# Hybrid decoder step: the second parts of the compression's rows come last, one operand pair lies lowest, one store moves to SP

## The chip, the core and the metric

The kernel runs on one core of a Trainium2 chip. The metric is the device time of one execution in microseconds (us), the median of several runs. Within the core, TensorE (PE) multiplies, VectorE (DVE), ScalarE (ACT) and GpSimd (POOL) work on rows, and SyncE (SP) issues transfers (DMA). PE has a queue of its own for loading weights, shown as PEld. Each engine takes its instructions in order and waits for semaphores of others.

## The reference

One layer of a hybrid decoder for 512 prompt tokens and 8 samples of 8 new tokens with 4096 earlier positions each. What matters here:

```python
def compress(rows, w1, b1, w2, b2, pos):          # rows -> compressed keys or values
    ch = rows[:, :nch * 16].reshape(B, nch, 16, N_KV, HEAD_DIM)
    h_first  = einsum('bcpgd,pdh->bcgh', ch, w1[:16])
    h_second = einsum('bcpgd,pdh->bcgh', ch, w1[16:])
    h = h_first[:, :-1] + h_second[:, 1:] + (einsum('pd,pdh->h', pos, w1) + b1)
    return einsum('bcgh,hd->bcgd', silu(h), w2) + b2

q, k_cmp, v_cmp, ..., gates, z_att, u, z_ssm, g_merge = split(x @ w_in)
kc, vc = compress(all_k, ...), compress(all_v, ...)      # prompt and samples
o_att = gated sum of: attention to kc/vc, to 16 selected blocks, to the window
y = gelu(S5(u));  s = (y @ glu_w[0] + b0) * sigmoid(y @ glu_w[1] + b1)
merged = sigmoid(g_att) * ((o_att * silu(z_att)) @ w_att_out) \
       + sigmoid(g_ssm) * ((s * silu(z_ssm)) @ w_ssm_out)
x = layer_norm(ALPHA * x + merged @ w_o)
```

All is float32. The kernel gets this precision on PE by splitting an operand into a first part (rounded, names ending in h) and a second part (the rest, names ending in l), and adding three products: first x first, second x first, first x second.

## The kernel before

The input projection and the S5 branch come first. Then the prompt's attention is done in four tiles of 128 tokens (`prompt_tile`, i = 0 to 3), and beside the later ones the compression of the samples' cached rows begins. Then four windows of two samples each attend (`attend`, w = 0 to 3), with the rest of the compression beside windows 0 to 2. The gated linear unit and the output projection of the S5 branch (`ssm_out`) run beside window 3. The attention's projection, `w_o` and the layer norm (`output`) end the kernel.

**Compression.** POOL gathers cached rows by page (`gc`, L1091), DVE transposes them (`xt`, L892), and `first_layer` multiplies them by the weights `w1`. It is called for 16 half-blocks x 2 (keys, values), and each call makes four steps, 128 in all. A step splits a quarter of the rows: ACT copies the first part `evh` (L108, in `split`), DVE subtracts to get the second part `evl` (L121). There are two buffers of each (`self.evs`), used in turn. Then come 12 products into the accumulator `p_mm`, three for each of four (r, f), in the order of `mm3`: `evh` with `w1h` (L129), `evl` with `w1h` (L130), `evh` with `w1l` (L131). SiLU (`hs`, `hth`) and the second layer (`p_ca`, L1165 and L1173) follow each block, with `kc` and `vc` as the results.

**Prompt tile.** Scores `p_S`, softmax `P`, transposes `p_tr` of `P` (L135), ACT's copies `pt`, products `p_acc` (L1036, L1078). At the end DVE multiplies the accumulator by the gate rows, `ast` (L1084), and the rows are stored to `aD` in DRAM (L1085), which a later load reads back. `attend_setup` follows: `kn`, and a load of a constant `selt` by SP (L1217), which the products of the gates need (L1220).

**Output part.** `ssm_out` takes 32 loads of `y` (issued by SP, held behind `selt`'s load by `issue_after`), splits `y` into four pairs `ah`, `al` (ACT, DVE) and the weights `or` into `oh`, `ol`, and multiplies. Its pool "out" lies where buffers of the compression lay before. Buffers get their addresses in the order in which they are first asked for: `z`, `ring`, then the pairs 0 to 3. So a pair may have to wait for what was there: pair 0 lies over the last `hth` and the rows `gc`, pair 3 above it.

**What sets the order.** The program is written as generators that are woven by hand, but a planner then reorders all instructions on all engines by its own model of times, within the limits of data and buffers. So a small edit can move instructions all over the program, and the order of what runs must be looked at as it comes out.

Of the kernel before, what the change touches and what calls it, by code (L numbers as in the profile page):

```python
# [85 lines left out]
def rr(ap, pat, **kw):  # L86
    return ap.rearrange(pat, **kw)


class Hybrid:  # L90
# [899 lines left out]
    def prompt_tile(self, i, KT, kczs, vcp, bt):  # L990

        nc, pp = self.nc, self.pp
# [4 lines left out]
        q0 = i * 128  # L997
        n = q0 + 128
        bv = bt[:]
        acc = self.psum("acc", [128, 512])  # L1000
        gr = self.grp
        for br in range(2):
# [21 lines left out]
            for kt in range(i + 1):  # L1024
# [10 lines left out]
                for g in range(2):  # L1035
                    mm = nc.tensor.matmul(acc[gr[g]], self.kvn[:, kt, c0 + g * 64:c0 + (g + 1) * 64], PTs[g][:], start=br == 0 and kt == 0,  # L1036
                                          stop=False, skip_group_check=True)
# [44 lines left out]
        st = pp.tile([128, 4, 128], F, name="ast", tag="ast", bufs=1)  # L1082
        nc.sync.dma_start(st[:], rr(self.zD[0:4], "r p t -> p r t")[:, :, q0:q0 + 128])
        V.tensor_tensor(st[:], rr(acc[:], "p (r q) -> p r q", r=4), st[:], op=OP.mult)  # L1084
        nc.scalar.dma_start(self.aD[:, :, q0:q0 + 128], st[:])  # L1085


    def gather(self, out, cache, idx):
# [55 lines left out]
    def first_layer(self, kv, h, x, acc):  # L1144

        for k2 in range(4):
            self.evn += 1
            xt = self.evs[self.evn % 2]
            self.split(xt[0][:, :, :, 1:129], xt[1][:, :, :, 1:129], x[:, 2 * k2:2 * k2 + 2])
            for r in range(2):  # L1150
                for f in range(2):
                    wj = 8 * f + 2 * k2 + r
                    to, at, n = (126, 0, 130) if h and f else (128 * h, 1 + f, 128)
                    self.mm3(acc[:, :, to:to + n], (self.w1s[kv][0][:, wj, :], self.w1s[kv][1][:, wj, :]),
                             (xt[0][:, r, :, at:at + n], xt[1][:, r, :, at:at + n]),
                             h == 0 and wj == 0, h == 1 and wj == 15, skip_group_check=True)
            yield

    def second_layer(self, kv, sl, out):
# [366 lines left out]
    def ssm_out(self):  # L1526

        nc, A, pd = self.nc, self.A, self.pd
        V, G = nc.vector, nc.gpsimd
        TT, TS, ST = V.tensor_tensor, V.tensor_scalar, V.scalar_tensor_tensor  # L1530
        self.halves = [slice(h * 288, h * 288 + 288) for h in range(2)]

        self.scratch("z")
        self.ring()
        for ct in range(4):
            self.pair(ct)
        self.weight_tiles()
        bg = pd.tile([128, 2, 4], F, name="bg")
        with nc.allow_non_contiguous_dma("bias"):
            nc.sync.dma_start(bg[:], rr(A["ssm_glu_b"], "k (t p) -> p k t", p=128))  # L1540
        TS(bg[:, 1], bg[:, 1], 0.5, None, op0=OP.mult)
        gh, gl = [], []
        for ct in range(4):
            y = self.py.tile([128, TOK], F, name="y", tag="y", bufs=4)
            ys = rr(self.yD[ct * 8:ct * 8 + 8], "g (t c) n -> g c t n", t=8)
            for g in range(8):
                with self.tc.issue_after(self.selt_dma.ins):
                    nc.sync.dma_start(rr(y[g * 16:(g + 1) * 16], "c (t n) -> c t n", t=8), ys[g])
            hi, lo = self.pair(ct)
            self.split(rr(hi, "p (n t) -> p t n", t=8), rr(lo, "p (n t) -> p t n", t=8), rr(y[:], "p (t n) -> p t n", t=8))  # L1550
            gh.append(hi)
            gl.append(lo)

        sh, sl = [], []
        gw = rr(A["ssm_glu_w"], "k (t p) c -> p k t c", p=128)
        for ct in range(4):
            c = slice(ct * 128, (ct + 1) * 128)
            hi, lo = self.weights([(gw[:, 0, :, c], 4), (gw[:, 1, :, c], 4)])
            z, th, ln = self.scratch("z"), self.scratch("th"), self.scratch("ln")
            nc.sync.dma_start(z[:], self.zD[4 + ct])  # L1560
            for s in self.halves:
                for k in (1, 0):
                    p = self.bank()
                    for t in range(4):
                        self.mm3(p[:, :288], (hi[:, 4 * k + t], lo[:, 4 * k + t]), (gh[t][:, s], gl[t][:, s]), t == 0, t == 3)
                    if k:
                        self.act(th[:, s], p[:, :288], AF.Tanh, scale=0.25, bias=bg[:, 1, ct:ct + 1])
                    else:
                        self.act(ln[:, s], p[:, :288], AF.Identity, scale=0.5, bias=bg[:, 0, ct:ct + 1])
                    yield  # L1570
            ST(ln[:], th[:], 1.0, ln[:], op0=OP.add, op1=OP.mult)
            G.tensor_tensor(ln[:], ln[:], z[:], op=OP.mult)
            hi, lo, _ = self.ring()
            self.split(hi, lo, ln[:])
            sh.append(hi)
            sl.append(lo)

        ws = rr(A["w_ssm_out"], "(t p) c -> p t c", p=128)
        self.merged = []
        for c2 in range(4):  # L1580
            self.merged += self.ring(F)[0:2]
            hi, lo = self.weights([(ws[:, :, (2 * c2 + u) * 128:(2 * c2 + u + 1) * 128], 4) for u in range(2)])
            for u in range(2):
                ct = 2 * c2 + u
                if ct == 0:
                    self.glu_dma = self.wdma
                tg = self.scratch("tg")
                nc.sync.dma_start(tg[:], self.gD[8 + ct])
                for s in self.halves:
                    p = self.bank()  # L1590
                    for t in range(4):
                        self.mm3(p[:, :288], (hi[:, 4 * u + t], lo[:, 4 * u + t]), (sh[t][:, s], sl[t][:, s]), t == 0, t == 3)
                    ST(self.merged[ct][:, s], tg[:, s], 1.0, p[:, :288], op0=OP.add, op1=OP.mult)
                    yield
# [136 lines left out]
```

## Time and profile before

| what | value |
|---|---|
| time, median of 3 runs | 892.15 us (891.99 to 892.65) |
| profiled execution, its time | 889.58 us |
| profiled execution, span from first to last instruction | 887.8 us |
| PE busy | 849.6 us, 96% |
| DVE busy | 568.8 us, 64% |
| ACT busy | 426.2 us, 48% |
| mean granted TensorE clock | 0.981 of full speed |

The profile shows one execution. Busy times are sums over the span; PE's products are pipelined, so a product's own duration is longer than the distance to the next one. All start times below are microseconds from the start of the span. The time and the span differ by 1.8 us, which lie around the program.

### The profile page before, as it was taken

How to read it: one execution, taken by the hardware profiler on the slowest of the kernel's cores; microseconds unless marked ns; L12 is line 12 of the kernel's file. 1: busy time of each engine (PE TensorE's matmuls, PEld its weight loads, DVE VectorE, ACT ScalarE, POOL GpSimd, SP SyncE). 2: the span in 40 equal slices, each digit the busy share in tenths (PEclk: the TensorE clock that was granted, in tenths of full speed). 3: DMA queues.
4: the chain of work that ended last, by engine and by line, in shares of the span. 5: the costliest groups of instructions: out<-in, count | busy, mean ns of one | idle time of the engine just before them, and what ended most of it. 6: DMA issues, size and time to landing. Idle time of an engine off the chain costs nothing.

```text
span 887.8 us, 18479 instructions
## 1 busy us (share of the span) xinstructions
PE 849.6 (96%) x7276; PEld 747.8 (84%) x7276; DVE 568.8 (64%) x1559; ACT 426.2 (48%) x876; POOL 196.0 (22%) x249
## 2 busy tenths in 40 slices
PE   8999999999999988999989999999999979999996
PEld 8999999999999967787757878787878758889885
DVE  3469973855354479988627767766764463448784
ACT  4224462223254365768535656555555565545420
POOL 0322719300042211121211323241321101200000
PEclk9999999999999979999979999999999989999999
DMA  8385526365687352323457746383726164849331
GB/s 279 95 201 165 148 67 193 113 203 150 208 247 239 135 133 96 120 96 120 148 182 216 264 164 261 120 313 116 285 97 238 61 236 145 283 129 277 109 107 48
DMA packets 116039, 151.03 MB, mean 170 GB/s; under 512 B 29352, under 2 KB 93224, under 8 KB 111600
## 3 DMA queue, kind: packets, MB, share of 16 engines
q1 hardware_dynamic: 89072, 65.02, 25.6%
q0 software_dynamic: 17824, 80.16, 25.2%
q10 hardware_dynamic: 9056, 4.67, 1.8%
q8 instruction: 57, 0.93, 0.4%
q14 instruction: 30, 0.25, 0.1%
HBM read 134.02 MB, written 19.93 MB: 173 GB/s over the span
## 4 chain that ended last, share of the span: by engine, by line
PE 65%; DVE 11%; DMA 7%; issue 5%; POOL 4%; ACT 4%; SPq 3%; POOLq 0%; DVEq 0%; ACTq 0%
PE p_mm L130 11%; PE p_mm L129 10%; PE p_mm L131 10%; PE p_tr L135 7%; PE p_S L1237 4%; PE p_ca L129 3%; PE p_ca L131 3%; PE p_ca L130 3%; DVE xt L892 2%; PE p_acc L1246 2%; DMA gc<-in_cache_kv_cmp,idx 2%; PE p_acc L1036 2%; DMA relx<-in_rel_bias 1%; DMA wraw<-in_w_in 1%; DVE evl L121 1%
## 5 line engine op out<-in xcount | busy, mean ns | idle before, releaser
L130 PE MATMUL p_mm<-evl,w1h 128*128 128x256 f32 (+1 forms) x512 | 153.8, 300 | 6.3 <-DVE evl L121 6.2
L129 PE MATMUL p_mm<-evh,w1h 128*128 128x256 f32 (+1 forms) x512 | 151.1, 295 | 1.1 <-ACT w1h L108 0.6
L131 PE MATMUL p_mm<-evh,w1l 128*128 128x256 f32 (+1 forms) x512 | 148.2, 290 | 0.9 <-DVE w1l L121 0.9
L121 DVE TENSOR_TENSOR evl<-xt,evh 128x512 fp32r<-128x512 f32 x128 | 87.0, 684 | 52.1 <-ACT evh L108 51.7
L130 PEld LDWEIGHTS p_mm<-evl,w1h 128*128 128x128 f32 x512 | 98.7, 193 | 24.8 <-DVE evl L121 13.1
L108 ACT ACTIVATE evh<-xt 128x512 fp32r<-128x512 f32 x128 | 80.1, 628 | 79.7 <-PE p_mm L131 75.2
L1091 POOL DMA_INDIRECT gc<-in_cache_kv_cmp,idx x64 | 65.5, 1024 | 206.7 <-DVE xt L892 188.9
L129 PEld LDWEIGHTS p_mm<-evh,w1h 128*128 128x128 f32 x512 | 98.9, 193 | 8.7 <-ACT kt L108 2.4
L131 PEld LDWEIGHTS p_mm<-evh,w1l 128*128 128x128 f32 x512 | 98.6, 193 | 5.8 <-issue 4.1
L892 DVE STREAM_TRANSPOSE xt<-gc 128x256 f32<-128x256 f32 x256 | 90.5, 410 | 5.2 <-DMA gc<-in_cache_kv_cmp,idx 4.6
L131 PE MATMUL p_mm<-xTh,wlo 128*128 128x288 f32 x272 | 81.0, 298 | 0.0
L130 PE MATMUL p_mm<-xTl,whi 128*128 128x288 f32 x272 | 81.0, 298 | 0.0
L129 PE MATMUL p_mm<-xTh,whi 128*128 128x288 f32 x272 | 80.9, 298 | 0.0
L108 ACT ACTIVATE pt<-p_tr 128x512 f32<-128x512 f32 x76 | 43.5, 591 | 29.3 <-PE p_tr L135 29.2
L341 DVE TENSOR_TENSOR wlo<-wraw,whi 128x512 fp32r<-128x512 f32 (+1 forms) x56 | 37.5, 728 | 25.4 <-ACT whi L108 25.4
L1091 POOL DMA_INDIRECT g<-in_cache_kv_slc,idx x32 | 32.6, 1018 | 92.9 <-PE p_acc L1246 65.7
L108 ACT ACTIVATE kt<-p_tr 128x512 f32<-128x512 f32 x72 | 40.7, 594 | 24.2 <-PE p_tr L135 24.2
L130 PEld LDWEIGHTS p_mm<-xTl,whi 128*128 128x128 f32 x272 | 51.3, 189 | 0.2 <-issue 0.2
L129 PEld LDWEIGHTS p_mm<-xTh,whi 128*128 128x128 f32 x272 | 51.3, 189 | 0.2 <-issue 0.2
L108 ACT ACTIVATE whi<-wraw 128x2048 fp32r<-128x2048 f32 (+2 forms) x24 | 37.1, 1563 | 29.9 <-DMA wraw<-in_w_in 9.4
L131 PEld LDWEIGHTS p_mm<-xTh,wlo 128*128 128x128 f32 x272 | 51.4, 189 | 0.0
L135 PE MATMUL p_tr<-cst,P 128*128 128x128 f32 x304 | 47.1, 284 | 0.6 <-ACT P L108 0.5
(527 smaller groups left out, 2105.4 us busy)
## 6 DMA issues: line engine op xcount, KB each, us to landing
wraw<-in_w_in SPq DMA_DIRECT2D x11, 1024.0 KB
wraw<-in_w_in SPq DMA_DIRECT2D x10, 512.0 KB
gD<-zst POOLq DMA_DIRECT2D x16, 288.0 KB, 3.2
tg<-gD SPq DMA_DIRECT2D x16, 288.0 KB
wn<-in_state_win_kv POOLq DMA_DIRECT2D x4, 1024.0 KB, 6.2
wor<-in_w_o SPq DMA_DIRECT2D x8, 512.0 KB
out<-in_state_win_kv SPq DMA_DIRECT2D x8, 504.0 KB
wraw<-in_w_in SPq DMA_DIRECT2D x3, 1056.0 KB
```

The costliest lines, as they stand in the source:

```text
L108: return self.nc.scalar.activation(out, in_, func, **kw)
L121: eng.tensor_tensor(lo, src, hi.bitcast(F), op=OP.subtract)
L129: mm(out, lhi, rhi, start=start, stop=False, **kw)
L130: mm(out, lhi, rlo, start=False, stop=False, **kw)
L131: mm(out, llo, rhi, start=False, stop=stop, **kw)
L135: return self.nc.tensor.transpose(out, in_, self.ident[:k, :k])
L341: (eng or self.nc.vector).tensor_tensor(lo[:, kl, :n], w[:, kl, :n], hi[:, kl, :n].bitcast(F), op=OP.subtract)
L892: self.nc.vector.transpose(out=out, in_=in_)
L1036: mm = nc.tensor.matmul(acc[gr[g]], self.kvn[:, kt, c0 + g * 64:c0 + (g + 1) * 64], PTs[g][:], start=br == 0 and kt == 0, stop=False, skip ...
L1091: self.nc.gpsimd.indirect_dma_start(out=rr(out, "c s v g d -> c (s v g d)"), out_offset=None, in_=src, in_offset=bass.IndirectOffsetOnAxis ...
L1237: mm = self.nc.tensor.matmul(out[r], self.qb[:, w, r], keys[b], start=True, stop=True)
L1246: self.nc.tensor.matmul(acc[r], PT[:, r], vals(b)[:, g * 64:(g + 1) * 64], start=start, stop=stop, skip_group_check=True)
```

## The change

It has three parts. In `first_layer` the 12 products of a step are written in another order: four of `evh` with `w1h`, four of `evh` with `w1l`, then four of `evl` with `w1h`. The products themselves are the same. In `ssm_out` the pair 3 (`ah3`, `al3`) is asked for first, so it has the lowest address in the pool, over weights of the first layer, and pairs 0 to 2 follow behind `z` and `ring`; pair 0 then lies over the rows `gc` alone. In `prompt_tile` the store of the last tile's rows (i == 3) is issued by SP and not by ACT.

```diff
--- before.py
+++ after.py
@@ -1082,7 +1082,7 @@
         st = pp.tile([128, 4, 128], F, name="ast", tag="ast", bufs=1)
         nc.sync.dma_start(st[:], rr(self.zD[0:4], "r p t -> p r t")[:, :, q0:q0 + 128])
         V.tensor_tensor(st[:], rr(acc[:], "p (r q) -> p r q", r=4), st[:], op=OP.mult)
-        nc.scalar.dma_start(self.aD[:, :, q0:q0 + 128], st[:])
+        (nc.sync if i == 3 else nc.scalar).dma_start(self.aD[:, :, q0:q0 + 128], st[:])
 
 
     def gather(self, out, cache, idx):
@@ -1147,13 +1147,15 @@
             self.evn += 1
             xt = self.evs[self.evn % 2]
             self.split(xt[0][:, :, :, 1:129], xt[1][:, :, :, 1:129], x[:, 2 * k2:2 * k2 + 2])
-            for r in range(2):
-                for f in range(2):
-                    wj = 8 * f + 2 * k2 + r
-                    to, at, n = (126, 0, 130) if h and f else (128 * h, 1 + f, 128)
-                    self.mm3(acc[:, :, to:to + n], (self.w1s[kv][0][:, wj, :], self.w1s[kv][1][:, wj, :]),
-                             (xt[0][:, r, :, at:at + n], xt[1][:, r, :, at:at + n]),
-                             h == 0 and wj == 0, h == 1 and wj == 15, skip_group_check=True)
+
+            for wp, xp in ((0, 0), (1, 0), (0, 1)):
+                for r in range(2):
+                    for f in range(2):
+                        wj = 8 * f + 2 * k2 + r
+                        to, at, n = (126, 0, 130) if h and f else (128 * h, 1 + f, 128)
+                        self.nc.tensor.matmul(acc[:, :, to:to + n], self.w1s[kv][wp][:, wj, :], xt[xp][:, r, :, at:at + n],
+                                              start=h == 0 and wj == 0 and wp + xp == 0, stop=h == 1 and wj == 15 and xp == 1,
+                                              skip_group_check=True)
             yield
 
     def second_layer(self, kv, sl, out):
@@ -1530,9 +1532,10 @@
         TT, TS, ST = V.tensor_tensor, V.tensor_scalar, V.scalar_tensor_tensor
         self.halves = [slice(h * 288, h * 288 + 288) for h in range(2)]
 
+        self.pair(3)
         self.scratch("z")
         self.ring()
-        for ct in range(4):
+        for ct in range(3):
             self.pair(ct)
         self.weight_tiles()
         bg = pd.tile([128, 2, 4], F, name="bg")
```

The planner's order changes with it in many places. The names: `evh_4031`, `evh_4035` are the two buffers; `p_mm` is the accumulator; lines from 1156 on are shifted by two or three in the new file.

On PE, a step of the first layer right behind the second layer in front of window 0. Before (the first three of its 12 products, behind the second layer's last):

```order
L1165 MATMUL p_ca<-hs,w_1271 64x255 [waits DVE_49]
L1165 MATMUL p_ca<-hs,w_1271 64x255
L129 MATMUL p_mm<-evh_4035,w1h_4003 128x2x128 [waits Activation_49]
L130 MATMUL p_mm<-evl_4036,w1h_4003 128x2x128
L131 MATMUL p_mm<-evh_4035,w1l_4004 128x2x128
```

and now (the whole step, behind the same):

```order
L1167 MATMUL p_ca<-hs,w_1271 64x255 [waits DVE_49]
L1167 MATMUL p_ca<-hs,w_1271 64x255
L1156 MATMUL p_mm<-evh_4035,w1h_4003 128x2x128 [waits Activation_49]
L1156 MATMUL p_mm<-evh_4035,w1h_4003 128x2x128 x3
L1156 MATMUL p_mm<-evh_4035,w1l_4004 128x2x128 x4
L1156 MATMUL p_mm<-evl_4036,w1h_4003 128x2x128 x4
```

The second buffer's part is needed at the ninth product of the step and not at the second; the first part's last use is the eighth.

On PE, the last prompt tile, from the transposes of its first two softmax pieces on. Before, with first-layer products between:

```order
L135 MATMUL p_tr<-cst,P_4481 128x128 [waits PE_49,Activation_49]
L135 MATMUL p_tr<-cst,P_4451 128x128 [waits PE_49]
L135 MATMUL p_tr<-cst,P_4451 128x128 x3
L135 MATMUL p_tr<-cst,P_4481 128x128 [waits DVE_49] x3
L130 MATMUL p_mm<-evl_4032,w1h_4001 128x2x128 [waits DVE_49]
L131 MATMUL p_mm<-evh_4031,w1l_4002 128x2x128
L129 MATMUL p_mm<-evh_4031,w1h_4001 128x2x128
```

and now:

```order
L135 MATMUL p_tr<-cst,P_4451 128x128 [waits PE_49,Activation_49]
L135 MATMUL p_tr<-cst,P_4451 128x128 [waits DVE_49] x2
L1036 MATMUL p_acc<-pt,kvn 64x512 [waits Activation_49]
L1036 MATMUL p_acc<-pt,kvn 64x512
L135 MATMUL p_tr<-cst,P_4451 128x128 [waits DVE_49]
L135 MATMUL p_tr<-cst,P_4481 128x128 [waits PE_49,Activation_49]
L135 MATMUL p_tr<-cst,P_4481 128x128 [waits DVE_49] x2
L135 MATMUL p_tr<-cst,P_4451 128x128 [waits PE_49]
L135 MATMUL p_tr<-cst,P_4451 128x128 x3
L135 MATMUL p_tr<-cst,P_4481 128x128 [waits DVE_49]
```

Before, 11 products of a first-layer step follow the first transposes; now scores and transposes of the tile follow one another and no first-layer product stands between. Counted over the whole order, 312 of the 1536 first-layer products stand ahead of the tile's last scores before and 432 now, and 120 and 0 between there and the products with `selt`. The last first-layer product stands in front of what ran at 710.9 us before, and now in front of what ran at 676.5 us.

On SP, around the load of `selt`. Before:

```order
L1083 DMA ast<-zD 128x4x128 [waits DMAHW3_49,DMAHW2_49,DVE_49]
L1083 DMA ast<-zD 128x4x128 [waits DMAHW5_49,DMAHW4_49,DVE_49]
L1217 DMA selt<-cst 64x512 [waits DMAHW7_49,PE_49]
L1548 DMA y<-yD 16x8x72 [waits DMAHW0_49,PE_49]
L1548 DMA y<-yD 16x8x72 [waits DMAHW1_49]
```

and now:

```order
L1083 DMA ast<-zD 128x4x128 [waits DMAHW3_49,DMAHW2_49,DVE_49]
L1083 DMA ast<-zD 128x4x128 [waits DMAHW5_49,DMAHW4_49,DVE_49]
L1085 DMA aD<-ast 512x1x128 [waits DMAHW6_49,DVE_49]
L1219 DMA selt<-cst 64x512 [waits DMAHW7_49,PE_49]
L1551 DMA y<-yD 16x8x72 [waits DMAHW0_49,PE_49]
L1551 DMA y<-yD 16x8x72 [waits DMAHW1_49]
```

The store of the last tile's rows stands in front of the load of `selt`, and the 32 loads of `y` behind it.

The first products of the output part followed the last transposes of window 2 before (rows of `ah` with `oh`); they now follow scores of window 3's first keys. Counted over the order, from window 3's scores that ran at 770.4 us before to its end at 803.5 us, 163 products of the output part stood between its instructions before, and 12 stand there now, all behind its last `p_acc`.

## Rows read from the trace of the kernel before

**Rows 1.** Page, part 1: busy us of each engine (share), instructions.

```profile
PE 849.6 (96%) x7276; PEld 747.8 (84%) x7276; DVE 568.8 (64%) x1559; ACT 426.2 (48%) x876; POOL 196.0 (22%) x249
```

**Rows 2.** Single stretches: length, busy us by engine (instructions), PEclk, DMA share, GB/s.

```profile
340.00:414.00 74.00, 70.48 (x487) 57.08 (x487) 64.57 (x203) 48.52 (x112) 16.77 (x18) 1.00 0.35 111
414.00:457.40 43.40, 38.04 (x252) 27.85 (x250) 26.34 (x74) 24.91 (x52) 7.79 (x9) 0.98 0.41 124
455.60:466.00 10.40, 10.02 (x41) 8.03 (x41) 2.73 (x10) 2.42 (x4) 2.23 (x3) 0.51 0.99 352
769.80:803.50 33.70, 33.70 (x356) 28.85 (x355) 15.48 (x49) 12.23 (x23) 0.00 (x0) 1.00 0.62 194
```

**Rows 3.** Page, part 5, first layer: busy us, mean ns, idle before, releaser.

```profile
L130 PE MATMUL p_mm<-evl,w1h 128*128 128x256 f32 (+1 forms) x512 | 153.8, 300 | 6.3 <-DVE evl L121 6.2
...
L121 DVE TENSOR_TENSOR evl<-xt,evh 128x512 fp32r<-128x512 f32 x128 | 87.0, 684 | 52.1 <-ACT evh L108 51.7
...
L108 ACT ACTIVATE evh<-xt 128x512 fp32r<-128x512 f32 x128 | 80.1, 628 | 79.7 <-PE p_mm L131 75.2
...
L892 DVE STREAM_TRANSPOSE xt<-gc 128x256 f32<-128x256 f32 x256 | 90.5, 410 | 5.2 <-DMA gc<-in_cache_kv_cmp,idx 4.6
```

**Rows 4.** Timeline, inside a first-layer step: start us, us, engine, instruction.

```profile
483.62 0.28 PE L129 MATMUL p_mm<-evh,w1h 128*128 128x260 f32 x1
...
483.74 0.28 PE L130 MATMUL p_mm<-evl,w1h 128*128 128x260 f32 x1
```

**Rows 5.** Waits of PE and of its weight loads (PEld): total us, times, longest.

```profile
PE p_mm L129 <- ACT evh L108: 0.5, 1, 0.5
...
PEld p_mm L130 <- DVE evl L121: 13.1, 16, 1.5
PEld p_mm L130 <- issue: 6.6, 10, 0.8
```

**Rows 6.** Timeline, PE in the tail of the last prompt tile.

```profile
444.91 1.08 PE L1036 MATMUL p_acc<-pt,kvn 128*64 128x512 f32 x4 [0.25 <-ACT pt L108]
...
447.32 1.08 PE L1036 MATMUL p_acc<-pt,kvn 128*64 128x512 f32 x4 [0.31 <-ACT pt L108]
```

**Rows 7.** Chain that ended last, same tail: start us, us on the chain.

```profile
440.44 0.87 PE p_tr L135 x8
...
442.63 1.01 PE p_acc L1036 x4
```

**Rows 8.** Timeline, where the output part begins.

```profile
716.65 4.33 ACT L108 ACTIVATE ah<-y 128x576 fp32r<-128x576 f32 x4
...
720.78 2.00 ACT L108 ACTIVATE oh<-or 128x1024 fp32r<-128x1024 f32 x2
...
721.88 0.61 PE L129 MATMUL p_mm<-ah,oh 128*128 128x288 f32 x1 [4.66 <-ACT oh L108]
```

**Rows 9.** Timeline, end of the last prompt tile.

```profile
453.22 0.69 DVE L1084 TENSOR_TENSOR ast<-p_acc,ast 128x512 f32<-128x512 f32 x1 [6.84 <-PE p_acc L1078]
...
453.94 0.52 ACTq L1085 DMA_DIRECT2D aD<-ast  x1
...
454.50 0.47 ACT L108 ACTIVATE kc<-p_ca,kb 128x255 f32<-128x255 f32 x1 [2.46 <-DVE ml L1401]
...
455.03 0.66 PE L1173 MATMUL p_ca<-w,hs 128*128 128x64 f32 x4 [1.86 <-ACT kc L108]
...
455.62 1.26 PE L1220 MATMUL p_S<-gs,selt 64*128 64x24 f32 x5
```

**Rows 10.** Timeline of SP's queue, 425 to 485.

```profile
437.12 0.51 SPq L1217 DMA_DIRECT2D selt<-cst  x1
450.86 30.27 SPq L1548 DMA_DIRECT2D y<-yD  x32
```

**Rows 11.** Page, part 6: DMA issues, KB each, median us to landing.

```profile
gD<-zst POOLq DMA_DIRECT2D x16, 288.0 KB, 3.2
...
wn<-in_state_win_kv POOLq DMA_DIRECT2D x4, 1024.0 KB, 6.2
```

## The prediction

> **What bounds the kernel now.** I read five views in this order: busy time by engine, single stretches with their granted clock, the costliest groups, the waits, and the timeline at the places that move. TensorE (PE) is busy for 849.6 of the 887.8 us of the span, VectorE (DVE) for 568.8 and ScalarE (ACT) for 426.2 [rows 1]. So PE is the bound, and the end can move in three ways only: PE waits less, PE works at a higher granted clock, or PE's idle time lies elsewhere. The number of products does not change. The clock is at full speed in most stretches (1.00 in 340 to 414); 455.6 to 466, behind a stretch in which PE was idle by turns, ran at 0.51, the lower of the two levels (1.2 GHz) [rows 2].
>
> The first layer is the largest single piece: three groups of 512 products, of which the costliest, 153.8 us with a mean of 300 ns, stands in the rows [rows 3]. The products overlap; in an undisturbed step a new one begins each 0.12 us (483.62, 483.74) [rows 4]. A step is one ACT copy (evh, 628 ns), one DVE subtraction (evl, 684 ns) and 12 products, 12 x 0.12 = 1.44 us of PE. Its second product needs evl. The reader is to see three waits here. ACT waits 75.2 us for products of earlier steps before it may overwrite evh, DVE waits 51.7 us for evh, and PE's products of evl wait 6.2 us for DVE [rows 3], their weight loads 13.1 us [rows 5]. The first two waits are not lost by themselves, because both engines have room; the last is lost on the bounding engine.
>
> **The change, part by part.**
>
> *Order of the products (edit 1).* Nothing is added; 512 x 3 products stay. PE now has eight products, 8 x 0.12 = 0.96 us, between the need for evh and the need for evl, where it had one, 0.12 us. DVE's subtraction of 0.684 us fits in 0.96 us, if it starts when evh is ready. So the waits for evl should nearly all go. The nearest rows give 6.2 us by PE and 13.1 us by the weight loads [rows 3, 5]; the load stands ahead of its product in line, so the truth lies between, and I take the middle: **-9.6 us** (-6.2 to -13.1). What is late next is evh itself, which cost PE only 0.5 us in the whole run [rows 5]; the new order also frees evh four products earlier (0.48 us), which helps ACT, and frees evl no earlier.
>
> The new instruction order shows more than that: the planner now runs the first layer ahead. Before the last prompt tile's last scores 432 first-layer products are done where 312 were, and behind them 0 where 120 were; the first layer is used up near 676 us of the old time instead of 711. This empties three places.
>
> First, the tail of the last prompt tile. In 414 to 457.4 PE is busy 38.04 of 43.4 us [rows 2], of which 120 x 0.12 = 14.4 us leave and 23.6 us stay. Where this tail is already uncovered, one round of products on P (p_acc) follows the last after 2.41 us (444.91, 447.32) [rows 6], though where the chain passes through PE alone eight transposes take 0.87 and the four p_acc parts 1.01 us [rows 7], 1.88 us in all; the other 0.53 us are the wait for ACT's copy. At 2.41/1.88 the 23.6 us would take 30.3 us, so the stretch shrinks by 13.1 and not by 14.4: +1.3 us. The ten steps go to the stretch ahead, where DVE is busy 64.57 of 74 us [rows 2]. A step costs DVE 0.684 + 2 x 0.41 = 1.50 us (two transposes of 410 ns [rows 3]), ten cost 15.0, and 9.4 are free: up to +5.6 us if all ten fall there. Part of the tail's idle time is idle now too, so I take **+1 us** (-2, if DVE's free time takes the ten steps and the tail keeps its present gaps, to 1.3 + 5.6 = +6.9).
>
> Second, the end of the last attention window. In 769.8 to 803.5 PE is busy without a gap, 33.70 of 33.70 us with 356 instructions [rows 2]. 163 of them are products of the output part that the new order puts earlier; at a pitch of about 0.13 us they are 21.5 us, and 12.2 us of attention stay. The waits for transposes and copies that these products hide become visible: by the same ratio 12.2 x 0.53/1.88 = 3.4 us. I take **+3.4 us** (0 to +7, twice that, because a softmax lies in the chain as well).
>
> *The fourth operand's buffers lowest (edit 2).* Before, ACT's four copies ah<-y run only from 716.65 to 720.98, two copies oh<-or behind them, and PE's first product of the output part waits 4.66 us for them [rows 8]. In the new order these copies wait for their loads alone, not for the last first-layer work, and stand earlier; but the same 4.33 + 2.00 us of ACT work [rows 8] still stands in a row ahead of the first product, in a place where the first layer is by now used up, and some 3.1 us of attention products lie beside it. The hole moves and is partly covered: **-2 us** (-4.7 to 0).
>
> *The last tile's rows stored by SP (edit 3).* Before, ACT issues this store for 0.52 us at 453.94 and then writes kc at 454.50; PE's L1173 waits 1.86 us for kc, and the gate products L1220 begin at 455.62 [rows 9]. Without the store ACT is free half a us earlier. But on SP the store now stands ahead of the load of selt, which went out at 437.12 [rows 10] and which L1220 needs. The store cannot go before ast ends, 453.22 + 0.69 = 453.91 [rows 9]; it takes 0.52 us and selt's own issue 0.51 us, so selt goes out at 454.43. Its landing is not in the trace; the nearest are a 288 KB transfer of 3.2 us and a 1 MB transfer of 6.2 us, by the median [rows 11]. So selt (128 KB) is there at 457.6 to 460.6, and L1220 starts 2.0 to 5.0 us later than now, with the scores, the second layer and the next first-layer steps queued behind it on PE. What waits on SP as well, the 32 loads of y (30.27 us of issue [rows 10]), is needed only at 716.65. Nothing is taken off for kc, since L1220 is the later of the two. I take a little more than the smaller transfer gives: **+2.5 us** (0, if it lands as soon as it is issued, to +5).
>
> The Trainium skill ("DMA: Bandwidth & Descriptors", section "Issuing engines are not separate DMA queues") says that starting transfers from several engines saves only the starting engine's own time. By that alone this edit would be worth the 0.52 us that ACT is given back, and the sum would be 3.0 us lower, 884.4 us; the trace has the 0.52 us, and it also has the load that the store would now hold.
>
> **Sum.** -9.6 + 1 + 3.4 - 2 + 2.5 = -4.7 us. It is made against the profiled run, 889.58 us (span 887.8 us and 1.8 us around it), which lies 2.57 us under the median of the runs; the same difference on the median of 892.15 us gives **887.4 us**. Behind 803.5 PE works on data of the whole attention, and I leave this stretch of 84.3 us (803.5 to the end of the span) as it is. About 0.2%, or 1.8 us, is what a measurement of this kernel can tell from no change.
>
> **Rivals.**
>
> *A larger gain.* The flow through the evh and evl buffers is the true limit of the middle of the kernel. For it: the 75.2 us that ACT waits for products [rows 3], and 6.6 us more before the weight loads of evl without a named cause [rows 5]. Against it: PE is busy 70.48 of 74 us in 340 to 414 [rows 2]. If all of 13.1 + 6.6 = 19.7 us goes instead of 9.6, the whole hole of 4.7 instead of 2, and the tail costs nothing: 887.4 - 10.1 - 2.7 - 1 = 873.6 us.
>
> *Slower.* The products used up early are the cover of the tail. DVE is the bound in the stretch ahead, so the ten steps do not go through faster there, and the tail runs bare. It decides at the 9.4 us that DVE has free in 340 to 414: if the ten steps with 15.0 us fall into it, +6.9 instead of +1. A longer bare tail also means that the clock falls sooner: 10.4 us at 0.51 in 455.6 to 466 cost some 5 us now [rows 2]; six us more at that level cost +3. 887.4 + 5.9 + 3 = 896.3 us.
>
> *It does not do what it says.* The evl waits go, but evh becomes the wait: ACT's copy starts only when the products two steps back are done, and nothing made that chain shorter except 0.48 us of release. If 4 us of the 9.6 come back so, the time is 887.4 + 4 = 891.4 us, no change that can be told.
>
> **How the numbers follow.** The forecast (883 to 890.3) has 0.48, the larger gain 0.12, no change 0.16, the slower one 0.24. So faster by over 0.2% has 0.60, within 0.2% 0.16, slower 0.24. The range reaches into both outer cases: down to 876, some two us short of the larger gain's full price, and up to 898, past the slower one's by the 2.5 us by which selt may land later than I take it; outside I leave under 0.1 on each side.
>
> **What would show it.** Right: the wait of L1156's products for evl falls from 6.2 to under 1 us; PE's idle time in the stretch of prompt tiles 1 to 3 falls; L1222 starts behind selt some 2 to 3 us after the tail's end; the wait of 4.66 us is shorter; in the last 30 us of the attention PE shows gaps of 0.3 to 0.6 us behind ACT's copies of transposes. Wrong: products that wait for evh by several us; an attention tail that is longer by over 8 us; a clock at half speed in places where it is full now; or a gain behind 803.5, which I have not counted.

## The result and the profile after

The changed kernel takes 897.8 us, the median of 15 runs (894.39 to 902.92); the kernel before, 892.53 us in 15 runs (889.34 to 896.17). The ratio is 1.006, with a 95% interval of 1.0042 to 1.0077: slower by some 5 us, where 887.4 us, faster by 4.7, was forecast. The time lies in the stated range; the direction was wrong.

The page of the changed kernel: busy time (first line) and the groups of the first layer, which answer to [rows 1] and [rows 3]; columns as there.

```profile
PE 849.8 (95%) x7276; PEld 749.4 (84%) x7276; DVE 570.1 (64%) x1559; ACT 428.4 (48%) x876; POOL 195.5 (22%) x249
...
L108 ACT ACTIVATE evh<-xt 128x512 fp32r<-128x512 f32 x128 | 80.0, 629 | 79.8 <-PE p_mm L1156 68.2
L121 DVE TENSOR_TENSOR evl<-xt,evh 128x512 fp32r<-128x512 f32 x128 | 86.4, 680 | 37.8 <-PE p_mm L1156 17.7
...
L1156 PE MATMUL p_mm<-evl,w1h 128*128 128x256 f32 (+1 forms) x512 | 90.2, 296 | 0.5 <-DVE evl L121 0.4
L1156 PE MATMUL p_mm<-evh,w1h 128*128 128x256 f32 (+1 forms) x512 | 87.6, 292 | 1.1 <-ACT w1h L108 1.1
L1156 PE MATMUL p_mm<-evh,w1l 128*128 128x256 f32 (+1 forms) x512 | 87.1, 289 | 0.0
```

The wait for evl is 0.4 us where it was 6.2, so the first step of the forecast did what it said. PE's busy time is the same (849.8 and 849.6 us), and the span is 896.0 us and not 887.8: PE stands still 8 us more. The waits of PE by cause, total us, times, longest us:

```profile
PE p_S L1222 <- DMA selt<-cst: 7.9, 1, 7.9
PE p_tr L135 <- ACT P L108: 6.1, 3, 2.5
...
PE p_mm L129 <- ACT oh L108: 2.5, 1, 2.5
...
PE p_mm L1156 <- DVE evl L121: 0.4, 1, 0.4
```

One wait is as long as the whole loss: 7.9 us for selt, which was 0. The place, in the timeline (answers to [rows 9] and [rows 10]):

```profile
457.08 0.45 ACT L108 ACTIVATE kc<-p_ca,kb 128x255 f32<-128x255 f32 x1
...
458.23 0.66 PE L1175 MATMUL p_ca<-w,hs 128*128 128x64 f32 x4
458.35 0.69 DVE L1084 TENSOR_TENSOR ast<-p_acc,ast 128x512 f32<-128x512 f32 x1 [12.09 <-PE p_acc L1078]
...
459.07 0.62 SPq L1085 DMA_DIRECT2D aD<-ast  x1
...
459.78 0.59 SPq L1219 DMA_DIRECT2D selt<-cst  x1
...
460.46 9.68 SPq L1551 DMA_DIRECT2D y<-yD  x9
...
466.78 1.90 PE L1222 MATMUL p_S<-gs,selt 64*128 64x24 f32 x8 [7.89 <-DMA selt<-cst]
```

The store leaves SP at 459.07, right behind ast; selt leaves at 459.78 (437.12 before) and its products start at 466.78, 7.0 us later. Nothing else is late: kc was written at 457.08 without waiting for a store. Single stretches of the changed kernel, with the columns of [rows 2]:

```profile
340.00:418.00 78.00, 76.81 (x549) 64.27 (x547) 70.85 (x214) 49.99 (x112) 17.21 (x18) 1.00 0.36 116
340.00:430.50 90.50, 89.31 (x636) 74.50 (x634) 81.10 (x241) 57.70 (x128) 21.18 (x22) 1.00 0.39 126
446.30:449.70 3.40, 3.37 (x11) 1.76 (x12) 0.00 (x0) 0.78 (x2) 0.00 (x0) 0.50 0.00 0
458.90:466.80 7.90, 0.02 (x1) 0.02 (x1) 0.60 (x6) 0.00 (x0) 3.58 (x4) 0.57 0.79 232
466.80:477.60 10.80, 10.42 (x42) 8.06 (x42) 2.44 (x9) 3.05 (x5) 0.00 (x0) 0.53 0.91 294
709.10:712.50 3.40, 2.85 (x12) 2.86 (x13) 3.40 (x4) 2.50 (x5) 0.00 (x0) 0.50 0.00 0
793.20:814.00 20.80, 15.95 (x202) 10.48 (x200) 6.99 (x34) 8.74 (x19) 0.00 (x0) 0.84 0.39 108
804.70:811.50 6.80, 5.98 (x137) 4.93 (x137) 1.47 (x8) 2.59 (x8) 0.00 (x0) 0.50 0.02 5
```

340 to 418 has PE busier than before, 76.81 of 78 us, and so it stays up to 430.5, where 432 first-layer products are done (89.31 of 90.5 us). 458.9 to 466.8 is empty. 466.8 to 477.6 runs at a granted clock of 0.53, nearly all of it the lower level, as 455.6 to 466 did before. Three short stretches, one in the tail of the last prompt tile (446.3 to 449.7), one where the output part begins (709.1 to 712.5) and one near the end of the last window (804.7 to 811.5), are at the lower level too. And the end of the last window, 793.2 to 814, has PE busy 15.95 of 20.8 us at 0.84, where in the kernel before all of 769.8 to 803.5 was busy (33.70 of 33.70 us) at 1.00.

**Where the time went.** Every instruction of the trace can be named by its place in the program's order. The table takes the same instruction in two kernels: its start, less its start in the kernel before, less the difference that was there at 320 us (up to there the products are the same, and the profiled run of the kernel before was 2.6 to 4.1 us ahead of these), and less the products of the first layer (0.119 us each, the distance inside a step) and of the output part (0.132) that one of them has done by then and the other has not. A number is time lost against the kernel before, up to that place.

| us in the kernel before, place | whole change | parts 1+2 | change, selt by POOL | part 3 alone | parts 1+2, evl fifth |
|---|---|---|---|---|---|
| 413, scores near the end of the last tile | -1.7 | -1.8 | -2.1 | +0.7 | -0.9 |
| 455, products of the first vc | -0.2 | +1.6 | -0.6 | -1.0 | -3.8 |
| 469, behind the gates | +7.8 | +1.6 | -1.7 | +6.2 | -5.2 |
| 676, first layer used up (whole change) | +1.8 | -4.4 | -7.6 | +5.3 | -8.5 |
| 728, behind the old hole at the output part | -2.9 | -8.2 | -11.5 | +5.4 | -5.2 |
| 770, last keys of window 3 | -3.5 | -8.8 | -12.0 | +5.2 | -2.4 |
| 803, end of window 3 | +4.0 | -3.5 | -4.1 | +6.0 | -1.8 |
| 875, near the end | +4.7 | -2.7 | -3.4 | +8.8 | +1.5 |

So in the whole change four things of 5 to 8 us meet: +8.0 at selt, -6.0 in windows 0 to 2, -4.7 where the output part begins, +7.5 at the end of window 3. With the smaller steps between them they come to +4.7, close to the 5.3 between the medians. The table rests on one profiled execution of each kernel. Parts 1 and 2 were profiled twice; the second time the same column reads -1.9, +2.7, +2.7, -3.0, -8.4, -9.0, -1.0, -0.3, up to 2.4 us from the first, so smaller differences between two columns tell nothing. The runs below take the four apart.

### The profile page after: what moved, and what is told of

The parts are those of the page before. It is cut to its first block, busy times and chain, and to the rows that moved or that the text cites. A ratio compares the mean times of both kernels' runs of the same rounds, so it can differ in the third digit from the quotient of the medians.

```text
span 896.0 us, 18586 instructions
## 1 busy us (share of the span) xinstructions
PE 849.8 (95%) x7276; PEld 749.4 (84%) x7276; DVE 570.1 (64%) x1559; ACT 428.4 (48%) x876; POOL 195.5 (22%) x249
## 4 chain that ended last, share of the span: by engine, by line
PE 68%; DVE 9%; DMA 9%; issue 5%; POOL 4%; ACT 3%; SPq 2%; DVEq 0%; ACTq 0%; POOLq 0%
PE p_mm L1156 19%; PE p_tr L135 8%; PE p_mm L129 4%; PE p_mm L131 4%; PE p_mm L130 4%; PE p_S L1239 4%; PE p_acc L1248 3%; PE p_ca L130 2%; PE p_ca L131 2%; PE p_ca L129 2%; DMA wraw<-in_w_in 2%; PE p_acc L1036 2%; DMA bt<-vD 1%; DMA g<-in_cache_kv_slc,idx 1%; PE p_mm L365 1%
## 5 line engine op out<-in xcount | busy, mean ns | idle before, releaser
L1156 PE MATMUL p_mm<-evl,w1h 128*128 128x256 f32 (+1 forms) x512 | 90.2, 296 | 0.5 <-DVE evl L121 0.4
L1156 PE MATMUL p_mm<-evh,w1h 128*128 128x256 f32 (+1 forms) x512 | 87.6, 292 | 1.1 <-ACT w1h L108 1.1
L1156 PE MATMUL p_mm<-evh,w1l 128*128 128x256 f32 (+1 forms) x512 | 87.1, 289 | 0.0
L1156 PEld LDWEIGHTS p_mm<-evl,w1h 128*128 128x128 f32 x512 | 72.8, 192 | 9.5 <-issue 4.4
L1156 PEld LDWEIGHTS p_mm<-evh,w1h 128*128 128x128 f32 x512 | 72.6, 193 | 8.8 <-issue 5.6
L1156 PEld LDWEIGHTS p_mm<-evh,w1l 128*128 128x128 f32 x512 | 72.8, 193 | 6.5 <-issue 6.1
L135 PEld LDWEIGHTS p_tr<-cst,P 128*128 128x128 f32 x304 | 35.9, 147 | 20.9 <-issue 11.3
```

Source lines behind the costliest of these rows:

```text
L135: return self.nc.tensor.transpose(out, in_, self.ident[:k, :k])
L1156: self.nc.tensor.matmul(acc[:, :, to:to + n], self.w1s[kv][wp][:, wj, :], xt[xp][:, r, :, at:at + n], start=h == 0 and wj == 0 and wp + xp ...
```

## The experiments

Theory A, formed from the two traces: the load of selt behind the store is what turns a small gain into a loss; the order of products gains in the flow (the first layer's steps from the split rows to the products) and pays at the bare end of window 3, where no independent products are left to fill PE's waits. Rival B: the order of products is the loss, and the store is neutral.

**Each part alone, and the first two together.** The diffs are the three hunks shown with the change, one at a time. The planner's order on PE depends on the first part alone: with it 432 first-layer products stand ahead of the last tile's scores and 396 products of the output part ahead of window 3's last keys, without it 312 and 222, whatever the others do. The ratios and their intervals are those on record; they are not the quotients of the medians beside them, and differ from these by up to 0.24%. Three chips were used, and each run is compared with the kernel before on its own chip: 893.46 us (median) beside the three parts and the first run of parts 1 and 2, 906.97 us beside those that say so, 892.88 us beside the rest.

Part 1:

> Only the products' order of the first layer is changed (the fourth pair's address and the store stay as before). Theory A, read from the two traces: the order of products gains some 8 us in the flow of the first layer, loses some 3 us in the tail of the last prompt tile and some 8 us at the end of the last attention window, and gains about 5 us where the output part begins; the load of selt behind the store costs some 6 us and is no part of it. So 890 to 893 us here, a product's wait for evl under 1 us, and the gate products with selt not waited for. Rival B: the loss of the whole change comes from the order of products, since it uses up the first layer early, and the store is neutral: 896 to 899 us here.

892.98 us, ratio 1.0001 (0.9976 to 1.0026). Theory A's figure: the order alone is neutral, no loss. In its trace the wait for evl is 0.4 us and there is none for selt. Counted as in the table it stands at -4.0 at 676, -6.9 at 728, -7.5 at 770 and -0.6 at 803: the order alone gains 2.9 us where the output part begins, with a wait for oh of 3.4 us and not 4.7, and loses 6.9 at the end of window 3.

Part 2:

> Only the fourth operand's buffers lie lowest. The order on PE is nearly that of the kernel before. Theory A: the copies of ah may start a little earlier than 716.65, the hole of 4.66 us shrinks by 0 to 3 us, the time is 890 to 892.5 us. Rival B: nothing that can be told, 892.5 us. Rival C: the pair lies over weights still in use, its copies wait for the last products of the keys' first layer, 893 to 896 us.

892.81 us, 1.000 (0.998 to 1.002). Nothing that can be told, rival B. PE's order is that of the kernel before, and the wait for oh stays 4.7 us: the address alone does not shrink it.

Part 3:

> Only the store of the last tile's rows goes from ACT to SP. Theory A: the load of selt is issued behind the store at about 454.5 us of the span instead of 437, lands 7 to 10 us after that, and the gate products start some 8 us after kc's products; 6 us are lost there, and the time is 897 to 899 us. Rival B: the wait for selt takes the place of time in which the half-speed clock would have been paid anyway or is made good in the next window, 892 to 894 us.

901.44 us, 1.0113 (1.0081 to 1.0145): slower than even theory A said. Its timeline at the place:

```profile
458.99 0.61 SPq L1085 DMA_DIRECT2D aD<-ast  x1
...
459.70 0.59 SPq L1217 DMA_DIRECT2D selt<-cst  x1
...
466.31 1.90 PE L1220 MATMUL p_S<-gs,selt 64*128 64x24 f32 x8 [7.50 <-DMA selt<-cst]
```

The picture of the changed kernel, in the old order of products: selt goes out at 459.70 and its products start at 466.31. 7.2 of the 8.8 us of the table are lost here (-1.0 to +6.2). Another 2.8 us are lost behind 803, where the planner's order of the output part also differs from the kernel before; they were not followed.

Parts 1 and 2:

> The change without its third part: the store stays on ACT. Theory A: 6 us less than the whole change, 891 to 893 us, and the gate products are ready as in the kernel before. Rival B: the store is neutral, 896 to 899 us.

890.3 us, 0.9973 (0.9953 to 0.9993). The store is the loss. What it costs ACT is seen here again, PE's rows at the place:

```profile
459.94 1.12 PE L1175 MATMUL p_ca<-w,hs 128*128 128x64 f32 x4 [1.86 <-ACT kc L108]
460.98 1.26 PE L1222 MATMUL p_S<-gs,selt 64*128 64x24 f32 x5
```

The products of vc wait 1.86 us for kc behind the store, and the gates' products follow at once. Run again on the third chip, it had 0.9985:

> Parts one and two again, on the same chip as the two runs above, as what they are compared with: a ratio of 0.995 to 0.999 to the kernel before.

891.89 us, 0.9985 (0.9964 to 1.0005). Between part 1 alone (1.0001) and both, the intervals overlap: that the address of the fourth pair is worth something is not shown by the times. In the traces the wait for oh is 3.4 us with part 1 alone and 2.5 with both, in either execution.

**The store on SP, and selt out of its way.** The whole change, with one word more:

```diff
-        self.selt_dma = nc.sync.dma_start(rr(selt[:], "p q r -> p (q r)"), A["cst2"][0:64, a:b])
+        self.selt_dma = nc.gpsimd.dma_start(rr(selt[:], "p q r -> p (q r)"), A["cst2"][0:64, a:b])
```

> The whole change, but POOL issues the load of selt, ahead of its first gather of selected rows; the store stays on SP and the order on PE is that of the changed kernel. Theory A (the load held by the store costs what the change loses): selt has landed before its products, their wait of 7.9 us goes to 0, kc is not held either, and the time is 888 to 891 us, 7 to 9 us under the changed kernel's. Rival B (the wait only takes the place of other idle time or of transfers that fill the queues there): 894 to 898 us.

898.03 us, but on a chip on which the kernel before took 906.97: 0.9916 (0.9887 to 0.9945). Again on the third chip:

> The whole change with selt on POOL again, on the same chip: 0.990 to 0.995 to the kernel before, 0.3 to 0.5% under the kernel with parts one and two alone, because neither kc nor selt waits for the store (1.9 us and 0.5 us there). If it is not under it, the gain seen on the other chip was that chip's.

887.17 us, 0.9926 (0.9899 to 0.9954). Its timeline at the place, and the stretch behind:

```profile
439.52 0.58 POOL L1219 DMA_DIRECT2D selt<-cst  x1 [17.31 <-PE p_S L1050]
...
458.01 0.62 SPq L1085 DMA_DIRECT2D aD<-ast  x1
...
459.16 1.05 PE L1222 MATMUL p_S<-gs,selt 64*128 64x24 f32 x4
```

```profile
458.00:470.00 12.00, 11.69 (x64) 9.87 (x65) 4.95 (x22) 4.25 (x8) 3.41 (x4) 0.72 0.92 330
```

POOL issues selt at 439.52, it has landed 2.5 us later, the store leaves SP at 458.01, and the gates' products run at 459.16 with no wait. The order of the first layer's products, the address and the store's engine are the change's own; what differs is the engine and with it the time of selt's issue, so the late load is what costs: 1.006 against 0.9926. PE does not stand still here, for selt or for kc, and 458 to 470 ran at a granted clock of 0.72, where the kernel before, in which PE had waited 1.86 us for kc, had 0.51 in 455.6 to 466.

The other way out, the store on POOL, with parts 1 and 2:

```diff
-        (nc.sync if i == 3 else nc.scalar).dma_start(self.aD[:, :, q0:q0 + 128], st[:])
+        (nc.gpsimd if i == 3 else nc.scalar).dma_start(self.aD[:, :, q0:q0 + 128], st[:])
```

> Parts one and two, and the last tile's store is issued by POOL, so that neither ACT's kc nor SP's load of selt stands behind it; the first gather of selected rows stands behind it. Theory A: the wait of 1.86 us for kc goes and nothing comes in its place, 888 to 890 us, 1 to 2 us under the kernel with parts one and two alone (890.3). Rival B: the gathers are late by the store and window 0 pays it back, 890 to 893 us.

900.78 us beside 906.97 for the kernel before: 0.9934 (0.9913 to 0.9954). Theory A: neither kc nor selt is held, and the gathers behind the store take no harm that can be told.

**The bare end of window 3.** The last 48 products of the output part are made to wait for a copy of keys in the second half of window 3, with parts 1 and 2, and in a second kernel with the store on POOL as well:

```diff
+                if w == 3 and name == 's1' and gi == 0:
+                    self.hold = done_at
...
-                self.weave(self.attend(3, store), steps, 32, 4)
+                self.weave(self.attend(3, store), steps, 32, 8)
...
-                        self.mm3(p[:, :288], ...
+                        one = self.mm3(p[:, :288], ...
+                        if t == 0 and c2 >= 3:
+                            self.after(one, self.hold)
```

The second hunk starts the output part's pieces four steps of window 3 later in the program as written. In what runs it shows nowhere ahead of the hold: PE's order is that of parts 1 and 2 up to there.

> Parts one and two; the last 48 products of the output part are made to wait for a copy of the keys in the second half of window 3, so that they lie beside its end. Theory A (the end of the last window runs bare, 5 us lost there against the kernel before): 48 x 0.13 = 6.3 us of products cover it, the loss halves, 887 to 889 us. Rival B: the bare end is bound by the gathers of rows or by the softmax, and the products that are held leave a hole in front of it, 890 to 892 us.

> The store by POOL and the 48 held products together. Theory A: the two gains add, 885 to 888 us, some 1% under the changed kernel and 0.6% under the kernel before. Rival B: 890 us, since neither place is what bounds the time.

911.0 us, 1.0045 (1.0021 to 1.0068), and 907.76 us, 1.0012 (0.999 to 1.0034), on the chip of the slower kernel before. Against the same kernels without the hold, it costs 0.6 to 0.7% (the first, by ratios from different chips) and 0.8% (the second, on one chip): rival B. The first of them in its timeline, and two stretches there:

```profile
797.09 2.88 PE L136 MATMUL p_tr<-cst,g 128*128 128x128 f32 x12 [4.79 <-DMA g<-in_cache_kv_slc,idx]
...
818.01 1.09 PE L136 MATMUL p_tr<-cst,P 128*128 128x128 f32 x8 [2.38 <-ACT P L108]
```

```profile
790.00:810.00 20.00, 14.58 (x110) 10.80 (x111) 2.92 (x11) 4.26 (x9) 2.12 (x4) 0.83 0.57 200
810.00:830.00 20.00, 15.80 (x206) 11.88 (x206) 7.98 (x32) 7.42 (x16) 0.00 (x0) 0.83 0.37 104
```

PE reaches the transposes of the last gathered keys early and waits 4.79 us for the gather; then, behind the held products, the softmax is no less bare (2.38 us). The two kernels with the store on POOL, both on this chip, say the same: waits of 4.74 us for the gather and 2.38 for the softmax with the hold, 0.84 and 1.98 without. In the changed kernel the products that are done early had covered that gather, down to this wait of 1.07 us at 797.00, and the softmax is what is left uncovered:

```profile
797.00 1.06 PE L135 MATMUL p_tr<-cst,g 128*128 128x128 f32 x8 [1.07 <-DMA g<-in_cache_kv_slc,idx]
...
802.10 1.15 ACT L108 ACTIVATE P<-P,nms 128x1024 f32<-128x1024 f32 x1 [2.38 <-DVE nms L1290]
...
803.39 1.09 PE L135 MATMUL p_tr<-cst,P 128*128 128x128 f32 x8 [1.98 <-ACT P L108]
...
805.52 1.08 PE L1248 MATMUL p_acc<-g,pt 128*32 128x64 f32 x32 [1.03 <-ACT pt L108]
```

So the cover, the stock of independent products, is one: 48 products that move to the end are missing in front of it. The end is not simply a hole that can be filled; the theory's second half was wrong in that.

**The size of the step.** Parts 1 and 2 with the three kinds in another order, so that evl is needed at the fifth product (and evh is then in use up to the twelfth, as in the kernel before):

```diff
-            for wp, xp in ((0, 0), (1, 0), (0, 1)):
+            for wp, xp in ((0, 0), (0, 1), (1, 0)):
```

> Parts one and two, but in each step the four products of evl with w1h stand in the middle (evh with w1h, evl with w1h, evh with w1l), so that evl is needed 4 x 0.12 = 0.48 us after evh and not 0.96. The planner then runs the first layer ahead by far less: 316 and not 432 products ahead of the last tile's scores (312 before), 276 and not 396 products of the output part ahead of the last keys of window 3 (222 before). Theory A (the flow gains by the hidden subtraction, the run-ahead costs at the bare ends): the wait for evl is some 1 to 3 us and not 6.2, the end of window 3 costs 2 us and not 5, and the ratio to the kernel before is 0.992 to 0.996, as good as with evl last or better. Rival B (the gain comes from the run-ahead itself, which fills idle places of the windows): 0.997 to 1.002.

> As the run before, with the store on SP and the load of selt on POOL ahead of its gathers. Theory A: another 0.2 to 0.4% under it, a ratio of 0.988 to 0.993. Rival B: equal to the kernel with evl last and selt on POOL.

894.8 us, 1.0033 (1.001 to 1.0057), and, with selt on POOL, 892.51 us, 0.9992 (0.9968 to 1.0016). By the times theory A fails in both. The first lies just past rival B's range. The second is 0.7% above the kernel with evl last and selt on POOL (0.9926), the intervals apart, so there rival B fails too: the order with evl last is the better one. The trace of the first says where; PE's waits, and the stretch behind the start of the output part:

```profile
PE p_mm L129 <- ACT oh L108: 3.7, 1, 3.7
PE p_mm L1156 <- DVE evl L121: 2.5, 5, 0.7
```

```profile
715.80:722.00 6.20, 6.20 (x25) 5.93 (x26) 2.86 (x4) 2.34 (x4) 0.00 (x0) 0.51 1.02 381
```

The table's last column is better than any up to 676 us (-8.5; the second kernel stands at -10.9 there), with little run-ahead. So the gain does not need the run-ahead: windows 0 to 2 give 4.7 us (-3.8 to -8.5) where parts 1 and 2 gave 6.0, even with a wait of 2.5 us for evl left, and the tile's tail gains 2.9 where it cost 3.4. And the end of window 3 costs 0.6 us (-2.4 to -1.8) and not 5 to 8, less even than theory A said. But where the output part begins 3.3 us are lost (-8.5 to -5.2) instead of 4 gained: PE stands 3.7 us before the first of its products, as the kernel before did 4.66, and then runs 6.2 us at 0.51. Another 2.8 us go between 728 and 770 and 3.3 behind 803; these were not followed. In the changed kernel the same four copies and two weight copies by ACT,

```profile
704.32 4.42 ACT L108 ACTIVATE ah<-y 128x576 fp32r<-128x576 f32 x4
...
708.52 2.01 ACT L108 ACTIVATE oh<-or 128x1024 fp32r<-128x1024 f32 x2
...
709.64 0.61 PE L129 MATMUL p_mm<-ah,oh 128*128 128x288 f32 x1 [2.48 <-ACT oh L108]
```

stood beside the scores of window 3, and the wait was 2.48 us. Read from these traces, a run-ahead that uses up the first layer early lets the output part begin early; that is the gain it buys, and the bare end is its price.

## Why the prediction was wrong

**Waits for evl (-9.6).** The mechanism held: 6.2 us became 0.4. Flow gained 1.7 us up to the last tile's scores and 6.0 in windows 0 to 2, together -7.7, inside the stated bounds. The weight loads' wait for evl, the upper bound, fell from 13.1 to 2.0 us.

**Tail of the last tile (+1, -2 to +6.9).** In the table the tail costs 1.5 us with kc's wait gone and 3.4 with it (parts 1 and 2, -1.8 to +1.6). The size came out, but not by the mechanism, so that is luck. The waits for ACT's copies `pt`, which the term priced, are 2.5 us in all and were 2.0. What is new is a wait for the softmax,

```profile
444.55 1.09 PE L135 MATMUL p_tr<-cst,P 128*128 128x128 f32 x8 [2.48 <-ACT P L108]
```

where PE waited for P only 0.5 us in all before, and behind it 3.4 us at the lower level (446.3 to 449.7), 1.7 us lost. The count of 312 is also not that of the tile's last scores: the last two score blocks ran at 431.5 and 432.0, behind 385 first-layer products. The 120 of the sum are those from 414 on. DVE had 81.10 of the 90.5 us up to 430.5, about its share before, and did not become the bound: PE was busy 89.31 of these 90.5. The rival that let DVE decide there named a time near the measured one, 896.3, by a mechanism that did not happen. Its second half, a clock that falls sooner, came in part: those 3.4 us, and behind the tile 17.1 us at the lower level (459.9 to 477.0) and not 10.2 (455.6 to 465.8), though 6.9 of the 17.1 lie in the wait for selt.

**selt behind the store (+2.5, 0 to +5).** This is the step that failed. The queue, the waiting product and the time of the issue (0.7 us behind the end of ast) came as described. The landing was priced by medians of two other transfers, 3.2 and 6.2 us [rows 11], and a little more than the smaller one taken; from issue to use it took 7.0 us, beyond both. The loss is 8.0 us in the table, and the gain on kc, about 2 us (the tail's 1.5 against 3.4), is what stands against it: behind the gates the whole change stands 6.2 us above parts 1 and 2 (+7.8 against +1.6), where 2.5 was forecast.

The trace of the kernel before had a nearer price. It has no landing of selt, as the prediction says, but it has the DMA packets: selt left at 437.12, and its 0.13 MB ran on the hardware queue from 438.6 to 441.9, beside a gather's packets, 4.8 us from issue to the last. In the changed kernel the packets of the 256 KB store ran from 460.3 to 461.7; those of the first gather, which POOL issued at 459.08, began at 461.4; selt's ran among them from 463.2 to 465.9; and the DMA engines were busy 0.79 of the stretch 458.9 to 466.8. Issued by POOL ahead of the gathers, the same load had landed in 2.5 us. So it is slow in the company it now leaves with, and by these packets the gathers hold it at least as much as the store; no run took the two apart.

**Begin of the output part (-2, -4.7 to 0).** It gained 4.7, the whole of the bound: the wait went from 4.66 to 2.48 us, and the stretch at the lower level there from 6.8 us (718.4 to 725.2) to 3.4 (709.1 to 712.5), which is 1.7 us. But the term stood under the wrong edit. With the address alone the wait stays 4.7 us; with the order alone it is 3.4, and the place gains 2.9. The address adds 0.9 to that in the traces, too little for the times to show.

**End of window 3 (+3.4, 0 to +7).** It cost 7.5. The ratio 2.41/1.88 of a tile's tail was carried to a place where the chain is longer: gather, scores, softmax, transposes. The bound was twice the value, and the truth lay just past it. The waits there come to 4.1 us (1.07 for the gather, 1.98 for the softmax, 1.03 for the copy), and the clock fell too, which the term did not have: 6.8 us at the lower level (804.7 to 811.5), up to 3.4 us lost. The clock does not fall there each time. The place cost 5.3 us in an execution of parts 1 and 2 at 1.00 (795 to 806) and 8.0 in the other, with 6.8 us at the lower level (799.1 to 805.9).

The errors: +5.5 at selt, +4.1 at the end of window 3, +1.9 in the flow, +0.5 in the tail, -2.7 at the output part, and 0.1 in sum in stretches that were left as they were. That is 9.4 us, from -4.7 to +4.7. Most of it is a transfer and a chain that were priced by rows from other places. The time lies 0.2 us inside the stated range, whose upper end allowed for a later selt on top of the slower rival; that it is not outside is luck.

**The rivals.** "Does not do what it says" is refuted by the 0.4 us. "A larger gain" is half there: without the third part's price the change gains 0.7% (0.9926), some 7 us of the 18.5 that this rival named, and up to 728 us it gains 11.5.

The best version found is the change with selt issued by POOL: 0.9926 and 0.9916 of the kernel before on two chips, and by the two ratios (0.9926 and 1.006) 1.3% under the change. The store issued by POOL (0.9934) cannot be told from it.

## What to carry to other kernels

A store that must wait for the end of a stage, put into a queue of loads, holds every load behind it (here from 437 to 460 us), and the first of them may be the one that the next stage starts with; before a transfer is moved to another engine, list what stands behind it there and who needs that first. A load that can go out 20 us early should stand in a queue where nothing late is ahead of it. Cover is one stock: where an order uses independent products earlier, the places that they covered must be priced one by one, each by its own chain of gather, softmax and copies, since moving some back only moves the hole.

## What the runs showed of the hardware

A 128 KB load took 7.0 us from issue to use (459.78 to 466.78) beside a 256 KB store and gathers, and had landed in 2.5 us when it was issued at 439.52 ahead of the gathers.

After PE stood still 7.9 us for it, the next 10.8 us were granted 0.53; with the wait gone (selt by POOL) 12 us at the same place had 0.72. At the lower level 10.8 x 0.47 = 5.1 us are lost, with the wait gone 12 x 0.28 = 3.4: the wait costs its 7.9 us and some 1.7 more in the clock behind it. Two executions of one program, parts 1 and 2, differed by 6.8 us at the lower level at the end of window 3, and by 2.7 us of time lost there (8.0 and 5.3).

And one chip ran the same kernel before in 906.97 us and another in 892.88, 1.6% apart, with the ratio of the change with selt by POOL within its interval on both (0.9916 and 0.9926).
